# A feed-forward block in split-float32: up projection as Strassen products, down projection as a phase of its own

## The chip, the cores and the metric

The kernel runs on one core of a Trainium2 chip. The metric is the device time of one launch in microseconds (us). The kernel before takes 2258.77 us, the median of two runs (2258.36 and 2259.17).

## The reference

One residual layer over 512 tokens of 2048 channels, in float32: a token mixer with four groups of heads, its output projection and norm, and a feed-forward block. The change lies in the feed-forward and the norm ahead of it:

```python
x = x + rms_norm(y, post_mix_norm[l])
h = rms_norm(x, pre_ffn_norm[l])
y = conv_ffn(h, ffn_up[l], ffn_conv_w[l], ffn_conv_b[l], ffn_down[l])
x = x + rms_norm(y, post_ffn_norm[l])

def conv_ffn(h, up, conv_w, conv_b, down):
    hid = causal_dwconv(h @ up.astype(h.dtype), conv_w, conv_b)      # 3 taps over tokens
    gate, val = jnp.split(hid, 2, axis=-1)                           # 5632 channels each
    return (jax.nn.gelu(gate) * val) @ down.astype(h.dtype)
```

## The kernel before

Every float32 matrix is split into a high and a low part, and a product is three matmuls: high by high, high by low, low by high (`mul3`, L203-207). Weights come in blocks of 128x1024 floats, 512 KB, into one ring of three `raw` buffers (`load`, L160-169, on SP's queue); `split` (L144-158) casts the high part on ACT (`whi`, L155) and subtracts it on DVE (`wlo`, L156), each into four buffers.

The feed-forward has 44 tiles f of 128 gate channels and 44 of value channels. An up tile (`gemm_T`, `up_tile` L894) is 16 row tiles x 3 = 48 matmuls of 128x512 over two raw blocks, each of 8 row tiles of 128 columns, so 512 B in a row. DVE multiplies it by the norm's factor r2 (`fin`, L315), the convolution is one pass on ACT (L330) and two on DVE (L332), then gelu, the product with the gate (L908) and the split of the result into `fh` and `fl`, which stay in SBUF. The first tiles of both kinds go by halves of the tokens (`gemm_half`, L841: matmuls of 128x256), the first halves beside the norm of the last tokens. The norm's residual x1 is transposed on TensorE before r2 is known (L868 to L873); r2 is found meanwhile (`residual_norm`, L879).

The down projection is interleaved: after each group of four f (`up_group`, L901) it multiplies the group before it by ffn_down (`down_cols`, L918), 4 columns of 512 by 4 token tiles, and adds each PSUM bank to a sum in SBUF (L928). `finish` (L947) norms, adds the residual and stores. The order of the instructions on each engine is set by the tile framework's scheduler.

Of the kernel before, what the change touches and what calls it, by code (L numbers as in the profile page):

```python
# [45 lines left out]
# The order in which the mixers' parts are issued: what comes after a part of the DeltaNet fills in  # L46
# where that one waits.
# [9 lines left out]
def trunk(ctx: ExitStack, tc: tile.TileContext, x, xT, cols, rows, gdn_row, sgu_row, w_in, w_ba,  # L57
# [4 lines left out]
    # Slots of one tag are handed out in program order, so work that should run past other work  # L62
    # has tags of its own: G and mm for the DeltaNet, t, acc and fx for what fills in around it.
# [67 lines left out]
    a.activation(out=small([P, 1], "warm"), in_=half[:, 0:1], func=AF.Square)   # its table is loaded early  # L131
# [39 lines left out]
    def load_cols(w, c0):  # L171
        """128 columns, all rows; part (k) -> [P, 128] of hi and lo."""
# [20 lines left out]
    # One buffer of (hi, lo) activations, [channel, token tile, k, token], for h, y and h2 in turn.  # L193
# [9 lines left out]
    def mul3(p, lt, rt, first, last):  # L203
        """p += lt^T rt of (hi, lo) pairs."""
# [18 lines left out]
    def ones_sum(hi, lo, bank):  # L223
        """sums over the partitions of hi + lo, on every partition."""
# [16 lines left out]
    def col_sums(src, bank):  # L241
        """sums over the partitions, tokens on the partitions: [P, token tile]."""
# [19 lines left out]
    # lru_x goes along with the rows of x^T as they come  # L262
# [55 lines left out]
    def tanh_gate(t, zh):  # L318
        """zh holds z/2; gives z * sigmoid(z)."""
# [4 lines left out]
    def conv(dst, src, taps, bias=None):  # L324
        """causal depthwise convolution along the free axis; taps: columns, oldest first."""
# [28 lines left out]
    def softplus(dst, src, shape):  # L354
        """max(x, 0) + log1p(exp(-|x|)), the logarithm as 2 atanh(u / (2 + u))."""
# [112 lines left out]
        # decays  # L468
# [20 lines left out]
        # k k^T and (q k^T)^T  # L489
# [17 lines left out]
        # natural v  # L507
# [6 lines left out]
        # T = (I + M)^-1 by doubling, as its transpose  # L514
# [19 lines left out]
        # the 32nd power as the 16th's twice  # L534
# [10 lines left out]
        # w^T and u  # L545
# [42 lines left out]
    def gdn_norm(h):  # L588
        """x * rsqrt(mean(x^2) + eps) of x = o * rsqrt(P (|q|^2 + eps))"""
# [23 lines left out]
    def norm4(i, tiles):  # L613
        """rms_norm over 4 channel tiles with the i-th group's weight, in place."""
# [221 lines left out]
    # The first two tiles of the feed-forward go by halves of the tokens, the first half before the  # L836
    # last token tile is there.
    def load_up(f):
        return acc("pT"), load_cols(ffn_up, f * P)

    def gemm_half(i, p, wt):  # L841
        ts_ = slice(2 * i, 2 * i + 2)
        for k in range(KD):
            mul3(p[:, i * 2 * P:(i + 1) * 2 * P], wt(k), (act_hi[:, ts_, k, :], act_lo[:, ts_, k, :]),
                 k == 0, k == KD - 1)
# [3 lines left out]
    fetch_x(1)
    for t in range(NTT):  # L850
# [3 lines left out]
        wo_evac(p, t, c, pm)  # L854
        sr = small([P, 1], "sry")
# [5 lines left out]
        if t + 2 < NTT:  # L861
            fetch_x(t + 2)
        if t == NTT - 1:
            first = [gemm_half(0, *load_up(f)) for f in (0, NF)]
        for d in range(DC):
            pt = mm("pt2")
            for j in range(4):
                pe.transpose(pt[:, TS[j]], x1[t][d][:, TS[j]], ident)  # L868
            for j in range(4):
                hh, hl = act_N(4 * d + j, t)  # L870
                sc = col("pre_ffn", 4 * d + j)
                a.activation(out=hh, in_=pt[:, TS[j]], func=AF.Copy, scale=sc)  # L872
                v.scalar_tensor_tensor(out=hl, in0=pt[:, TS[j]], scalar=sc, in1=hh.bitcast(F32),  # L873
                                       op0=ALU.mult, op1=ALU.subtract)
# [1 line left out]
    r2b = new("rb", "r2b")  # L876
    r2 = const.tile([P, NTT], F32, name="r2")

    def residual_norm():  # L879
        for t in range(NTT):  # L880
            for c in range(DC):
                nc.sync.dma_start(out=x1d[TS[t], c * S:(c + 1) * S], in_=x1[t][c])
                junk = waste()
                a.activation(out=junk, in_=x1[t][c], func=AF.Square, accum_out=ss1[:, t, c:c + 1])  # L884
        sr2 = small([P, NTT], "sr2")
        v.tensor_reduce(out=sr2, in_=ss1, axis=mybir.AxisListType.X, op=ALU.add)
        col_rsqrt(r2, sr2, 1.0 / D)
        v.tensor_copy(r2b, to_row(r2, mm))
# [143 lines left out]
```

## Time and profile before

| what | value |
|---|---|
| median of the runs | 2258.77 us |
| span of the profiled execution | 2256.1 us |
| runs' median less the span (launch and end) | 2.7 us |
| TensorE (PE) busy | 2229.6 us, 99% |
| VectorE (DVE), ScalarE (ACT), GpSimd (POOL) busy | 1138.8, 753.2, 104.9 us |
| first matmul of the feed-forward (trace) | 800.72 us |
| last matmul (trace) | 2244.88 us |

All durations of the prediction are from the one profiled execution. In its rows `out<-in` are the program's names; PE is the matmul, PEld the weight load beside it; SPq is SP's DMA queue. Matmuls overlap in the records, so the price of one is read from start to start.

### The profile page before, as it was taken

What the parts mean: (1) busy time and instruction counts of PE and PEld (TensorE: products, weight loads), DVE (VectorE), ACT (ScalarE), POOL (GpSimd) and SP (SyncE); (2) the same over time, 40 slices, a digit from 0 to 9 for tenths busy, and PEclk for the clock granted to TensorE, in tenths of its full rate; (3) what the DMA queues carried; (4) which work ended last, traced back from release to release, by engine and by line L of the source; (5) the groups of instructions that cost most, each with busy time, mean ns of one, the idle gap of its engine ahead of it and who ended that gap; (6) DMA issues with size and microseconds to landing.
All of it is one profiled execution on the core that took longest, in us unless ns stands there. A gap on an engine that the chain in (4) does not pass through costs nothing.

```text
span 2256.1 us, 25143 instructions
## 1 busy us (share of the span) xinstructions
PE 2229.6 (99%) x10260; PEld 1845.3 (82%) x10260; DVE 1138.8 (50%) x1518; ACT 753.2 (33%) x1061; POOL 104.9 (5%) x99
## 2 busy tenths in 40 slices
PE   7999999999999999999999999999999999999998
PEld 6788888888888888888888888888888888888886
DVE  8675453944452474433544445444444444444456
ACT  5464242522332363333223232222323232232323
POOL 6001000100100000000000000000000000000002
PEclk9999999999999999999999999999999999999999
DMA  6222222232243543333333332333333333333352
GB/s 206 72 78 76 66 75 75 78 82 75 84 145 98 168 126 99 94 94 103 90 107 94 96 100 86 106 97 94 103 94 94 98 97 94 103 94 101 96 187 103
DMA packets 308339, 227.13 MB, mean 101 GB/s; under 512 B 8832, under 2 KB 263552, under 8 KB 307712
## 3 DMA queue, kind: packets, MB, share of 16 engines
q1 hardware_dynamic: 303616, 217.15, 33.0%
q10 hardware_dynamic: 4608, 8.39, 1.1%
q8 instruction: 80, 1.31, 0.2%
q14 instruction: 35, 0.29, 0.0%
HBM read 217.12 MB, written 8.39 MB: 100 GB/s over the span
## 4 chain that ended last, share of the span: by engine, by line
issue 63%; PE 31%; ACT 2%; DVE 2%; POOL 1%; DMA 0%; SPq 0%; DVEq 0%; POOLq 0%; ACTq 0%
PE pT L205 5%; PE pT L206 5%; PE pT L207 5%; PE pwo L205 2%; PE pwo L206 2%; PE pwo L207 2%; PE ptt L445 1%; DVE act_lo L280 1%; PE pvs L207 1%; PE pvs L206 1%; PE pvs L205 1%; PE pp L445 1%; PE pss L571 1%; ACT waste L884 0%; DVE wlo L156 0%
## 5 line engine op out<-in xcount | busy, mean ns | idle before, releaser
L205 PE MATMUL pT<-act_hi,whi 128*128 128x512 f32 (+1 forms) x2016 | 781.8, 388 | 1.8 <-ACT act_hi L872 1.8
L206 PE MATMUL pT<-act_lo,whi 128*128 128x512 f32 (+1 forms) x2016 | 781.9, 388 | 0.0
L207 PE MATMUL pT<-act_hi,wlo 128*128 128x512 f32 (+1 forms) x2016 | 780.8, 387 | 0.0
L155 ACT CAST whi<-raw 128x1024 fp32r<-128x1024 f32 x378 | 398.0, 1053 | 1012.3 <-PE pT L206 626.4
L156 DVE TENSOR_TENSOR wlo<-raw,whi 128x1024 fp32r<-128x1024 f32 x378 | 464.5, 1229 | 417.2 <-ACT whi L155 415.7
L205 PEld LDWEIGHTS pT<-act_hi,whi 128*128 128x128 f32 x2016 | 378.5, 188 | 78.9 <-ACT act_hi L872 2.6
L206 PEld LDWEIGHTS pT<-act_lo,whi 128*128 128x128 f32 x2016 | 378.8, 188 | 76.5 <-issue 1.0
L207 PEld LDWEIGHTS pT<-act_hi,wlo 128*128 128x128 f32 x2016 | 378.8, 188 | 76.4 <-issue 1.0
L206 PE MATMUL pd<-wlo,fh 128*128 128x512 f32 x704 | 273.7, 389 | 0.0
L207 PE MATMUL pd<-whi,fl 128*128 128x512 f32 x704 | 273.7, 389 | 0.0
L205 PE MATMUL pd<-whi,fh 128*128 128x512 f32 x704 | 273.5, 389 | 0.0
L315 DVE TENSOR_TENSOR fin<-pT,r2b 128x512 f32<-128x512 f32 x88 | 60.8, 691 | 285.7 <-PE pT L207 285.7
L928 DVE TENSOR_TENSOR facc<-pd,facc 128x512 f32<-128x512 f32 x156 | 107.5, 689 | 132.5 <-PE pd L207 131.8
L206 PEld LDWEIGHTS pd<-wlo,fh 128*128 128x128 f32 x704 | 132.1, 188 | 27.5
L207 PEld LDWEIGHTS pd<-whi,fl 128*128 128x128 f32 x704 | 132.1, 188 | 27.4
L205 PEld LDWEIGHTS pd<-whi,fh 128*128 128x128 f32 x704 | 132.1, 188 | 27.4
L332 DVE SCALAR_TENSOR_TENSOR fcv<-fin,colt,fcv 128x511 f32<-128x511 f32 (+1 forms) x176 | 131.2, 747 | 3.0 <-ACT fcv L330 0.3
L206 PE MATMUL pwo<-wlo,act_hi 128*128 128x512 f32 x224 | 87.1, 389 | 0.0
L207 PE MATMUL pwo<-whi,act_lo 128*128 128x512 f32 x224 | 87.0, 389 | 0.0
L205 PE MATMUL pwo<-whi,act_hi 128*128 128x512 f32 x224 | 86.5, 389 | 0.0
L330 ACT ACTIVATE fcv<-fin,colt 128x512 f32<-128x512 f32 x88 | 71.3, 811 | 1.9 <-DVE fin L315 1.9
L911 ACT CAST fh<-fcv 128x512 fp32r<-128x512 f32 x44 | 27.3, 621 | 122.4 <-DVE fcv L908 122.4
(318 smaller groups left out, 1511.8 us busy)
## 6 DMA issues: line engine op xcount, KB each, us to landing
raw<-in_ffn_up_dram SPq DMA_DIRECT2D x176, 512.0 KB, 4.0
raw<-in_ffn_down_dram SPq DMA_DIRECT2D x88, 512.0 KB, 3.6
raw<-in_w_in_dram SPq DMA_DIRECT2D x86, 512.0 KB, 3.8
raw<-in_w_out_dram SPq DMA_DIRECT2D x32, 512.0 KB, 3.9
xs<-in_xT_dram SPq DMA_DIRECT2D x16, 256.0 KB, 5.3
xr<-in_x_dram ACTq DMA_DIRECT2D x16, 256.0 KB, 5.3
x1d<-yw SPq DMA_DIRECT2D x16, 256.0 KB, 3.6
act_hi<-x1d SPq DMA_DIRECT2D x4, 1024.0 KB, 10.5
```

Of the source, the lines that this page charges most:

```text
L155: a.copy(out=hi, in_=r)
L156: v.tensor_tensor(out=lo, in0=r, in1=hi.bitcast(F32), op=ALU.subtract)
L205: pe.matmul(p, lhsT=lt[0], rhs=rt[0], start=first, stop=False)
L206: pe.matmul(p, lhsT=lt[0], rhs=rt[1], start=False, stop=False)
L207: pe.matmul(p, lhsT=lt[1], rhs=rt[0], start=False, stop=last)
L280: v.scalar_tensor_tensor(out=hl, in0=blk(xs[j]), scalar=col("pre_mix", k), in1=hh.bitcast(F32), op0=ALU.mult, op1=ALU.subtract)
L315: v.tensor_tensor(out=t, in0=p, in1=m, op=ALU.mult)
L330: a.activation(out=dst, in_=src, func=AF.Identity, scale=taps[-1], bias=bias)
L332: v.scalar_tensor_tensor(out=dst[:, j:], in0=src[:, :S - j], scalar=taps[n - 1 - j], in1=dst[:, j:], op0=ALU.mult, op1=ALU.add)
L445: pe.matmul(p[:, TS[t]], lhsT=lhsT[:, TS[t]], rhs=rhs[:, TS[t]], start=True, stop=True)
L911: a.copy(out=ah, in_=vt)
L928: v.tensor_tensor(out=facc[t][c], in0=p, in1=facc[t][c], op=ALU.add)
```

## The change

**Up.** f = 0 to 2 stay plain. From f = 3 on, gate tile f and value tile 44 + f are one product of 2x2 blocks, and Strassen's scheme in its form with 15 additions makes it of 7 block products with 8 row tiles and 256 tokens each: 7 x 8 x 3 = 168 matmuls of 128x256. The four weight blocks are r11 (gate, upper rows), r21 and r22 (value, upper and lower), r12 (gate, lower). Of the four sums of weight blocks, DVE makes s1 = r21 + r22 and s2 = s1 + r11; the other two are made in place by DMAs on GpSimd's queue that read weight rows once more and add them to what stands in the buffer: r21 += gate upper, s2 += gate lower. Each of the 7 blocks is split.

```diff
+    def add_rows(dst, k0, f):
+        nc.gpsimd.dma_start(out=dst.rearrange("p (k n) -> p k n", n=P), accum_op=ALU.add,
+                            in_=ffn_up[k0 * P:(k0 + 8) * P, f * P:(f + 1) * P].rearrange("(k p) n -> p k n", p=P))
+    def up_pair(f):
+        r11, r21, r22, r12 = (load(ffn_up, k0, 8, ff * P, P) for ff, k0 in
+                              ((f, 0), (NF + f, 0), (NF + f, 8), (f, 8)))
+        s1, s2 = B("s1"), B("s2")
+        gs, vs = T("fg"), T("fv")
+        g1, g2, v1, v2 = gs[:, 0:H2], gs[:, H2:], vs[:, 0:H2], vs[:, H2:]
+        add(s1, r21, r22)
+        p1 = product(split(r11), "B11")
+        a.copy(out=v1, in_=p1)
+        add(s2, s1, r11)
+        p5 = product(split(s1), "T1")
+        add_rows(r21, 0, f)
+        p6 = product(split(s2), "T2")
+        add(g2, v1, p6)
+        p2 = product(split(r12), "B21")
+        add(g1, v1, p2)
+        add_rows(s2, 8, f)
+        p7 = product(split(r21), "T3")
+        add(v1, g2, p7)
+        add(v2, v1, p5)
+        add(g2, g2, p5)
+        p4 = product(split(r22), "T4")
+        add(v1, v1, p4)
+        p3 = product(split(s2), "B22")
+        add(g2, g2, p3)
+        gated(f, gs, vs, True)
```

`product` is 8 x `mul3` into a bank of 256 columns, `add` a DVE addition (L984 of the changed kernel), `gated` the convolution, gelu and product, whose result now goes to DRAM (`gd`) by a DMA on GpSimd's queue:

```diff
+        v.tensor_tensor(out=vt, in0=vt, in1=gt, op=ALU.mult)
+        nc.gpsimd.dma_start(out=gd[f * P:(f + 1) * P, :], in_=vt)
+    NPL = 3
...
+    for f in range(NPL, NF):
+        up_pair(f)
```

**Norm.** r2 is found for each token tile and multiplied in before the transposes; `fin` (L315) is gone. The transposed tiles are kept in float32 (`hT`), and DVE and ACT make the sums of activation blocks and their splits from them once, beside f = 1 and 2.

```diff
+        for d in range(DC):
+            a.activation(out=xr[t, d], in_=x1[t][d], func=AF.Copy, scale=r2[:, t:t + 1])
...
-    r2b = new("rb", "r2b")
...
-        s = ev(p, r2b, "fin")
```

**Down.** A phase of its own after all of up: the same 2112 matmuls of 128x512, in two halves of 22 f. The four token tiles of a column hold a PSUM bank each over all 22 f, so an addition in SBUF comes once per bank and not once per group. The first column of each half loads `gd` back and splits it.

```diff
+    for h in range(2):
+        gs = []
+        for c in range(DC):
+            banks = [bank("pd") for _ in range(NTT)]
+            by_k = NH // 2 if h == 0 or c < DC - 1 else 7
+            for i in range(by_k):
+                if c == 0:
+                    gs += [load_g(h * NH + 2 * i + n, 2 * i + n) for n in range(2)]
+                wt = weights(h, i, c)
+                for n in range(2):
+                    k = 2 * i + n
+                    for t in range(NTT):
+                        mul3(banks[t], cut(gs[k], TS[t]), wt[n], k == 0, k == NH - 1)
```

The mixers' buffers are freed before the feed-forward and taken over by a pool of 18 buffers of 1024 floats and 7 of 512; PSUM is regrouped into 8 equal banks. The ring of three `raw` buffers and the four of `whi` and `wlo` stay.

**Order on DVE.** Before, one value tile and one gate tile of the feed-forward, among them 4 splits of weights (`wlo`), in the middle of an up group:

```order
L156 TENSOR_TENSOR wlo_6604<-raw_6601,whi_6603 128x1024
L315 TENSOR_TENSOR fin_6522<-pT_6473,r2b_6212 128x512
L156 TENSOR_TENSOR wlo_6610<-raw_6607,whi_6609 128x1024
L332 SCALAR_TENSOR_TENSOR fcv_6524<-fin_6522,colt_75,fcv_6524 128x511
L332 SCALAR_TENSOR_TENSOR fcv_6524<-fin_6522,colt_75,fcv_6524 128x510
L908 TENSOR_TENSOR fcv_6524<-fcv_6524,fcv_6456 128x512
L912 TENSOR_TENSOR fl_6530<-fcv_6524,fh_6529 128x512
L156 TENSOR_TENSOR wlo_6676<-raw_6673,whi_6675 128x1024
L315 TENSOR_TENSOR fin_6594<-pT_6545,r2b_6212 128x512
L156 TENSOR_TENSOR wlo_6682<-raw_6679,whi_6681 128x1024
L332 SCALAR_TENSOR_TENSOR fcv_6596<-fin_6594,colt_75,fcv_6596 128x511
L332 SCALAR_TENSOR_TENSOR fcv_6596<-fin_6594,colt_75,fcv_6596 128x510
```

After, in the middle of the pairs, from the split of r12 (raw_11637) of one pair to the first sum of the next (s1_11877). raw_11633 is r21, raw_11635 is r22, raw_11631 was r11:

```order
L160 TENSOR_TENSOR wlo_11736<-raw_11637,whi_11735 128x1024
L336 SCALAR_TENSOR_TENSOR fcg_11620<-fg_11403,colt_75,fcg_11620 128x511
L336 SCALAR_TENSOR_TENSOR fcv_11625<-fv_11404,ncv_6206,fcv_11625 128x511
L336 SCALAR_TENSOR_TENSOR fcg_11620<-fg_11403,colt_75,fcg_11620 128x510
L160 TENSOR_TENSOR wlo_11767<-raw_11633,whi_11766 128x1024
L336 SCALAR_TENSOR_TENSOR fcv_11625<-fv_11404,ncv_6206,fcv_11625 128x510
L925 TENSOR_TENSOR fcv_11625<-fcv_11625,fcg_11620 128x512
L160 TENSOR_TENSOR wlo_11799<-raw_11635,whi_11798 128x1024
L984 TENSOR_TENSOR fg_11641<-fv_11642,pT2_11709 128x256
L160 TENSOR_TENSOR wlo_11829<-s2_11640,whi_11828 128x1024
L984 TENSOR_TENSOR fg_11641<-fv_11642,pB21_11739 128x256
L984 TENSOR_TENSOR s1_11877<-raw_11871,raw_11873 128x1024
```

What was a `wlo` every two or three short instructions is now a fixed sequence: three convolution steps stand between the split of r12 and that of r21, which waits for the accumulating DMA too; behind the split of r22 comes the next pair's s1, which reads a buffer that this split frees.

**Order on SP's and GpSimd's queues.** Before, SP's loads of up tiles; GpSimd's instructions from the norm before the feed-forward on (no DMAs):

```order
L166 DMA raw_6539<-in_ffn_up_dram 128x8x128
L166 DMA raw_6601<-in_ffn_up_dram 128x8x128
L166 DMA raw_6607<-in_ffn_up_dram 128x8x128
L166 DMA raw_6673<-in_ffn_up_dram 128x8x128
L166 DMA raw_6679<-in_ffn_up_dram 128x8x128
```

```order
L141 TENSOR_TENSOR ry_5599<-crs_5917,half_82 128x1
L141 TENSOR_TENSOR ry_5599<-crs_6031,half_82 128x1
L141 TENSOR_TENSOR r2_6213<-crs_6360,half_82 128x4
L141 TENSOR_TENSOR rf_15082<-crs_15391,half_82 128x1
L963 TENSOR_TENSOR facc_7398<-facc_7398,act_hi_90 128x512
L963 TENSOR_TENSOR facc_7542<-facc_7542,act_hi_90 128x512
```

After, the four loads of a pair on SP (r11, r21, r22, r12) and two of the next; GpSimd's queue at the same place:

```order
L170 DMA raw_11631<-in_ffn_up_dram 128x8x128
L170 DMA raw_11633<-in_ffn_up_dram 128x8x128
L170 DMA raw_11635<-in_ffn_up_dram 128x8x128
L170 DMA raw_11637<-in_ffn_up_dram 128x8x128
L170 DMA raw_11869<-in_ffn_up_dram 128x8x128
L170 DMA raw_11871<-in_ffn_up_dram 128x8x128
```

```order
L988 DMA raw_11395<-in_ffn_up_dram 128x8x128
L988 DMA s2_11402<-in_ffn_up_dram 128x8x128
L926 DMA gd_6205<-fcv_11387 128x512
L988 DMA raw_11633<-in_ffn_up_dram 128x8x128
L988 DMA s2_11640<-in_ffn_up_dram 128x8x128
L926 DMA gd_6205<-fcv_11625 128x512
L988 DMA raw_11871<-in_ffn_up_dram 128x8x128
L988 DMA s2_11878<-in_ffn_up_dram 128x8x128
```

A pair has four loads for three buffers: r12 takes that of its own r11, the next r11 that of r12, the next r21 and r22 those of r21 and r22. On GpSimd's queue each pair has the accumulate into r21, the one into s2, and the store of the pair's result, where before there was nothing.

## Rows read from the trace of the kernel before

**Rows 1.** The page: busy time by engine, slices of the span, granted clock.
```profile
PE 2229.6 (99%) x10260; PEld 1845.3 (82%) x10260; DVE 1138.8 (50%) x1518; ACT 753.2 (33%) x1061; POOL 104.9 (5%) x99
...
PE   7999999999999999999999999999999999999998
...
PEclk9999999999999999999999999999999999999999
```

**Rows 2.** Window table: span, then PE, PEld, DVE, ACT, POOL busy (count), clock.
```profile
1000.00:1200.00 200.00, 200.00 (x884) 165.59 (x883) 85.50 (x96) 59.52 (x70) 0.00 (x0) 1.00 0.34 98
```

**Rows 3.** Timeline of PE in the first halves: start, duration, instruction.
```profile
805.25 0.28 PE L205 MATMUL pT<-act_hi,whi 128*128 128x256 f32 x1
...
812.81 0.28 PE L205 MATMUL pT<-act_hi,whi 128*128 128x256 f32 x1
```

**Rows 4.** Waits of SP's queue: us in total, times, longest.
```profile
SPq L166 <- DVE wlo L156: 1796.3, 346, 18.0
```

**Rows 5.** Timeline of DVE in the feed-forward.
```profile
1114.65 1.23 DVE L156 TENSOR_TENSOR wlo<-raw,whi 128x1024 fp32r<-128x1024 f32 x1 [0.17 <-ACT whi L155]
1115.79 0.74 DVE L332 SCALAR_TENSOR_TENSOR fcv<-fin,colt,fcv 128x511 f32<-128x511 f32 x1
1116.51 0.69 DVE L928 TENSOR_TENSOR facc<-pd,facc 128x512 f32<-128x512 f32 x1
1117.11 0.74 DVE L332 SCALAR_TENSOR_TENSOR fcv<-fin,colt,fcv 128x510 f32<-128x510 f32 x1
```

**Rows 6.** The page's costliest groups: busy, mean ns of one, idle before.
```profile
L155 ACT CAST whi<-raw 128x1024 fp32r<-128x1024 f32 x378 | 398.0, 1053 | 1012.3 <-PE pT L206 626.4
...
L315 DVE TENSOR_TENSOR fin<-pT,r2b 128x512 f32<-128x512 f32 x88 | 60.8, 691 | 285.7 <-PE pT L207 285.7
...
L330 ACT ACTIVATE fcv<-fin,colt 128x512 f32<-128x512 f32 x88 | 71.3, 811 | 1.9 <-DVE fin L315 1.9
```

**Rows 7.** The page: queues (packets, MB, share); issues (count, KB, us to landing).
```profile
q1 hardware_dynamic: 303616, 217.15, 33.0%
q10 hardware_dynamic: 4608, 8.39, 1.1%
...
raw<-in_ffn_up_dram SPq DMA_DIRECT2D x176, 512.0 KB, 4.0
...
act_hi<-x1d SPq DMA_DIRECT2D x4, 1024.0 KB, 10.5
```

**Rows 8.** Timeline of all engines at one load: cast, subtraction, next issue.
```profile
1025.39 1.05 ACT L155 CAST whi<-raw 128x1024 fp32r<-128x1024 f32 x1 [0.77 <-PE pd L207]
...
1026.47 1.23 DVE L156 TENSOR_TENSOR wlo<-raw,whi 128x1024 fp32r<-128x1024 f32 x1 [7.81 <-ACT whi L155]
...
1027.73 0.37 SPq L166 DMA_DIRECT2D raw<-in_ffn_up_dram  x1
```

**Rows 9.** Timeline of the end: a power, the last matmul, the last store.
```profile
2244.32 0.55 POOL L141 TENSOR_TENSOR rf<-crs,half 128x1 f32<-128x1 f32 x1
...
2244.88 0.39 PE L207 MATMUL pd<-whi,fl 128*128 128x512 f32 x1
...
2252.78 0.33 SPq L967 DMA_DIRECT2D out_dram<-fm  x1
```

**Rows 10.** Timeline of PE from the first half product to the first whole.
```profile
800.72 0.28 PE L205 MATMUL pT<-act_hi,whi 128*128 128x256 f32 x1
...
813.53 1.91 PE L868 MATMUL pt<-ident,yw 128*128 128x128 f32 x16
815.93 0.39 PE L205 MATMUL pT<-act_hi,whi 128*128 128x256 f32 x1 [0.50 <-ACT act_hi L872]
...
830.70 0.39 PE L205 MATMUL pT<-act_hi,whi 128*128 128x512 f32 x1
```

**Rows 11.** The page: weight loads of the up tiles.
```profile
L205 PEld LDWEIGHTS pT<-act_hi,whi 128*128 128x128 f32 x2016 | 378.5, 188 | 78.9 <-ACT act_hi L872 2.6
```

More of the change, by code (lines that the diff above doesn't have):

```diff
@@ L802, in trunk @@
     ssy = const.tile([P, NTT, DC], F32, name="ssy")
+    x1b = [[None] * 2 for _ in range(NTT)]
     x1 = [[None] * DC for _ in range(NTT)]
@@ L819, in trunk, with held_rows @@
             wo_evac(pos[t], t, c, pm)
+    def held_rows(w, k0, c0, held):
+        h = sum((split(r, 1, (lambda n: B(n, F32R)) if held else None) for r in load_raw(w, k0, c0)), [])
+        return lambda i: tuple(side(t, i % 2) for t in h[i // 2])
     c = DC - 1
     pm = row_tile(0, c, "t")
-    spare = ["y"] * NBUF["y"] + ["o"] * NBUF["o"]
-    wts = [load_rows(w_out, order[4 * q], c * S, pick=None if q < 2 else lambda n: new(spare.pop(0), n, F32R))
-           for q in range(4)]
+    wts = [held_rows(w_out, order[4 * q], c * S, q >= 2) for q in range(4)]
     ry = const.tile([P, NTT], F32, name="ry")
+    r2 = const.tile([P, NTT], F32, name="r2")
     ss1 = const.tile([P, NTT, DC], F32, name="ss1")
@@ L843, in gemm_half @@
         for k in range(KD):
[L844 removed]
+            mul3(p[:, i * H2:(i + 1) * H2], wt(k), (act_hi[:, ts_, k, :], act_lo[:, ts_, k, :]),
                  k == 0, k == KD - 1)
         return p, wt
+    hT = [[None] * 2 for _ in range(NTT)]
     fetch_x(0)
[L849 removed]
     for t in range(NTT):
@@ L860, in trunk @@
                                    op0=ALU.mult, op1=ALU.add)
-        if t + 2 < NTT:
-            fetch_x(t + 2)
+            junk = waste()
+            a.activation(out=junk, in_=x1[t][d], func=AF.Square, accum_out=ss1[:, t, d:d + 1])
+            nc.sync.dma_start(out=x1d[TS[t], d * S:(d + 1) * S], in_=x1[t][d])
+        sr2 = small([P, 1], "sr2")
+        v.tensor_reduce(out=sr2, in_=ss1[:, t, :], axis=mybir.AxisListType.X, op=ALU.add)
+        col_rsqrt(r2[:, t:t + 1], sr2, 1.0 / D)
+        for d in range(DC):
+            a.activation(out=xr[t, d], in_=x1[t][d], func=AF.Copy, scale=r2[:, t:t + 1])
         if t == NTT - 1:
-            first = [gemm_half(0, *load_up(f)) for f in (0, NF)]
+            first = [gemm_half(0, acc("pT"), load_cols(ffn_up, f * P)) for f in (0, NF)]
         for d in range(DC):
@@ L877, in trunk @@
[L877 to L888, printed above, removed]
+                pe.transpose(pt[:, TS[j]], xr[t, d][:, TS[j]], ident)
@@ new lines, in trunk @@
+            if d % 2 == 0:
+                hT[t][d // 2] = B("hT")
+            h1 = side(hT[t][d // 2], d % 2)
+            o, _ = _OFF["pre_ffn"]
+            v.tensor_tensor(out=blk(h1), in0=blk(pt), op=ALU.mult,
+                            in1=colt[:, o + 4 * d:o + 4 * d + 4].rearrange("p (k o) -> p k o", o=1)
+                            .broadcast_to([P, 4, P]))
+            hh, hl = (u[:, t, 4 * d:4 * d + 4, :] for u in (act_hi, act_lo))
+            a.copy(out=hh, in_=blk(h1))
+            v.tensor_tensor(out=hl, in0=blk(h1), in1=hh.bitcast(F32), op=ALU.subtract)
@@ new lines, in trunk, with taps, gated @@
+    gd = dr.tile([DFF, S], F32, name="gd")
+    o_cv = _OFF["ffn_conv"][0] + 3 * NF
+    ncv = tp.tile([P, 3 * NF], F32, tag="ncv", name="ncv", bufs=1)
+    v.tensor_scalar_mul(ncv, colt[:, o_cv:o_cv + 3 * NF], -1.0)
+    def taps(f, minus=False):
+        if minus:
+            return [ncv[:, 3 * (f - NF) + i:3 * (f - NF) + i + 1] for i in range(3)]
+        return [col("ffn_conv", 3 * f + i) for i in range(3)]
+    def gated(f, gs, vs, minus):
+        gt = T("fcg")
+        conv(gt, gs, taps(f), bias=col("ffn_cb", f))
+        a.activation(out=gt, in_=gt, func=AF.Gelu_apprx_tanh)
+        vt = T("fcv")
+        conv(vt, vs, taps(NF + f, minus), bias=col("ffn_cb", NF + f))
+        v.tensor_tensor(out=vt, in0=vt, in1=gt, op=ALU.mult)
+        nc.gpsimd.dma_start(out=gd[f * P:(f + 1) * P, :], in_=vt)
@@ L916, in trunk @@
-    facc = [[None] * DC for _ in range(NTT)]
-    def down_cols(parts, c, after=None):
-        wts = [load_rows(ffn_down, gi * FG, c * S) for gi, _ in parts]
-        for t in range(NTT):
-            p = bank4(t)("pd")
-            for i, (_, act) in enumerate(parts):
-                gemm_N(p, lambda k, t: cut(act[k], TS[t]), 0, FG, wts[i], t, i == 0, i == len(parts) - 1)
-            if facc[t][c] is None:
-                facc[t][c] = G("facc")
-                a.copy(out=facc[t][c], in_=p)
-            else:
-                v.tensor_tensor(out=facc[t][c], in0=p, in1=facc[t][c], op=ALU.add)
-            if after is not None:
-                after(t, c)
@@ L932, in trunk @@
-    prev = last = None
-    for gi in range(NG):
-        prev, last = last, (gi, up_group(gi))
-        if prev is not None:
-            for c in range(DC if gi < NG - 1 else DC - 1):
-                down_cols([prev], c)
+    gated(0, first[0][0], first[1][0], False)
+    for j in range(2):
+        b11, b21, b12, b22 = hT[j][0], hT[j][1], hT[j + 2][0], hT[j + 2][1]
+        v.tensor_tensor(out=b22, in0=b22, in1=b12, op=ALU.subtract)
+        v.tensor_tensor(out=b12, in0=b11, in1=b12, op=ALU.subtract)
+        v.scalar_tensor_tensor(out=b11, in0=b11, scalar=-1.0, in1=b22, op0=ALU.mult,
+                               op1=ALU.subtract)
+        v.scalar_tensor_tensor(out=b21, in0=b11, scalar=-1.0, in1=b21, op0=ALU.mult,
+                               op1=ALU.subtract)
@@ new lines, in trunk @@
+    ext = {}
+    for q, t0, i in (("T1", 2, 0), ("T2", 0, 0), ("T3", 2, 1)):
+        ext[q] = [(B("eh", F32R), B("el", F32R)) for _ in range(2)]
+        for j in range(2):
+            for d in range(2):
+                src = side(hT[t0 + j][i], d)
+                eh, el = (side(u, j) for u in ext[q][d])
+                a.copy(out=eh, in_=src)
+                v.tensor_tensor(out=el, in0=src, in1=eh.bitcast(F32), op=ALU.subtract)
+    for f in range(1, NPL):
+        pg, pv = (gemm_T(ffn_up, ff * P) for ff in (f, NF + f))
+        gated(f, pg, pv, False)
@@ new lines, in trunk, with bank, moving @@
+    banks_end.close()
+    ps = ctx.enter_context(tc.tile_pool(name="ps2", bufs=1, space=PSUM, reuse_waits="tile"))
+    def bank(name):
+        return ps.tile([P, S], F32, tag="u", name=name, bufs=8)
+    for j in range(2):
+        src = blk(hT[j][1])
+        eh, el = (u[:, 2 + j, 0:8, :] for u in (act_hi, act_lo))
+        a.copy(out=eh, in_=src)
+        v.tensor_tensor(out=el, in0=src, in1=eh.bitcast(F32), op=ALU.subtract)
+    def moving(q, k):
+        if q in ext:
+            return tuple(u.rearrange("p (j k c) -> p j k c", j=2, k=4)[:, :, k % 4, :] for u in ext[q][k // 4])
+        t0, k0 = {"B11": (0, 0), "B21": (0, 8), "B22": (2, 8), "T4": (2, 0)}[q]
+        return tuple(u[:, t0:t0 + 2, k0 + k, :] for u in (act_hi, act_lo))
@@ new lines, in product, with add @@
+    def product(wt, q):
+        p = bank("p" + q)[:, 0:H2]
+        hi, lo = wt[0]
+        for k in range(8):
+            mul3(p, (hi[:, k * P:(k + 1) * P], lo[:, k * P:(k + 1) * P]), moving(q, k), k == 0, k == 7)
+        return p
+    def add(o, x, y):
+        v.tensor_tensor(out=o, in0=x, in1=y, op=ALU.add)
+    def add_rows(dst, k0, f):
+        nc.gpsimd.dma_start(out=dst.rearrange("p (k n) -> p k n", n=P), accum_op=ALU.add,
+                            in_=ffn_up[k0 * P:(k0 + 8) * P, f * P:(f + 1) * P].rearrange("(k p) n -> p k n", p=P))
@@ new lines, in trunk, with load_g @@
+    for f in range(NPL, NF):
+        up_pair(f)
+    NH = NF // 2
+    GAT = [(0, 0), (0, 1), (1, 0), (1, 1), (0, 2), (0, 3), (1, 2), (1, 3), (2, 2), (2, 3), (3, 2), (3, 3),
+           (2, 0), (2, 1), (3, 0), (3, 1)]
+    def load_g(f, i):
+        gr = T("graw")
+        nc.sync.dma_start(out=gr, in_=gd[f * P:(f + 1) * P, :])
+        if i < 16:
+            t, k = GAT[i]
+            hi, lo = (u[:, t, 4 * k:4 * k + 4, :].rearrange("p k c -> p (k c)") for u in (act_hi, act_lo))
+        else:
+            b = B("gb", F32R)
+            hi, lo = side(b, 0), side(b, 1)
+        a.copy(out=hi, in_=gr)
+        v.tensor_tensor(out=lo, in0=gr, in1=hi.bitcast(F32), op=ALU.subtract)
+        return hi, lo
@@ L940, in trunk, with weights @@
+    fb = [[B("facc") for _ in range(2)] for _ in range(NTT)]
+    facc = [[side(fb[t][c // 2], c % 2) for c in range(DC)] for t in range(NTT)]
+    pf = None
+    def weights(h, i, c):
+        hi, lo = split(load(ffn_down, h * NH + 2 * i, 2, c * S, S))[0]
+        return [(side(hi, n), side(lo, n)) for n in range(2)]
     ssf = const.tile([P, NTT, DC], F32, name="ssf")
     rf = const.tile([P, NTT], F32, name="rf")
-    pf = [row_tile(1, c, "t") for c in range(DC)]
-    x1r = [act_hi[:, t].rearrange("p k c -> p (k c)").bitcast(F32) for t in range(NTT)]
@@ L944, in trunk @@
-    for t in range(NTT):
-        nc.sync.dma_start(out=x1r[t], in_=x1d[TS[t], :])
     def finish(t, c):
@@ L967, in finish @@
             (nc.sync if d % 2 else nc.scalar).dma_start(out=out[TS[t], cs], in_=fd)
-    for c in range(DC - 1):
-        down_cols([last], c, finish)
-    down_cols([prev, last], DC - 1, finish)
+    for h in range(2):
[11 more added lines that the diff above has]
+                        mul3(banks[t], cut(gs[k], TS[t]), wt[n], k == 0, k == NH - 1)
+            if h == 1 and c == DC - 1:
+                x1r = []
+                for t in range(NTT):
+                    x1r.append((act_hi, act_lo)[t % 2][:, t // 2].rearrange("p k c -> p (k c)").bitcast(F32))
+                    nc.sync.dma_start(out=x1r[t], in_=x1d[TS[t], :])
+                wts = [weights(h, i, c) for i in range(by_k, NH // 2)]
+            for t in range(NTT):
+                if h == 1 and c == DC - 1:
+                    for i, wt in enumerate(wts):
+                        for n in range(2):
+                            k = 2 * (by_k + i) + n
+                            mul3(banks[t], cut(gs[k], TS[t]), wt[n], False, k == NH - 1)
+                if h == 0:
+                    a.copy(out=facc[t][c], in_=banks[t])
+                    continue
+                v.tensor_tensor(out=facc[t][c], in0=banks[t], in1=facc[t][c], op=ALU.add)
+                finish(t, c)
+        if h == 0:
+            pf = [row_tile(1, c, "t") for c in range(DC)]
 _ORDER = ["x", "xT", "cols", "rows", "gdn_row", "sgu_row", "w_in", "w_ba", "lru_wa", "lru_wx", "sgu_ws",
```

52 lines of the change are left out of this document (17 added, 35 removed).

## The prediction

> **What bounds the kernel now.** I read the page's busy shares and slices first: the matmul engine is busy 99% of the span, in every slice, at the top level of the granted clock, 2.4 GHz [rows 1]. DVE has half of its time free, ACT two thirds. So a change gains by fewer or shorter matmuls and loses by whatever makes TensorE wait. Next a window table inside the feed-forward, for the price of a matmul: 884 of 128x512 in 200 us, 226.3 ns each [rows 2]. Then the timeline of the one place with 128x256 matmuls: from 805.25 to 812.81 lie 63 of them, 0.120 us each [rows 3]. Half a matmul thus costs 0.53 of a whole one, which eats part of what Strassen saves. Last SP's waits: it waited 1796 us for DVE's `wlo` to free a `raw` buffer [rows 4]. The loads are tied to DVE by a ring of three buffers, which costs nothing today because TensorE has its weights early.
>
> **Matmuls.** Per f, two up tiles are 96 matmuls of 512 columns: 96 x 0.2263 = 21.72 us. A Strassen pair is 7 x 8 x 3 = 168 of 256 columns: 168 x 0.120 = 20.16 us. Over 41 pairs: 41 x 1.56 = **-64.0 us**. The down projection keeps 2112 matmuls of 128x512, and f = 0 to 2 keep theirs: 0.
>
> **DVE and ACT per pair.** From start to next start, DVE takes 1.15 us for a `wlo`, 0.72 for a conv step, 0.60 for a 512-column operation [rows 5]. After the change it has 7 `wlo`, 2 sums of 1024 elements, 4 conv steps, a product and 7 additions of 256 columns: 9 x 1.15 + 4 x 0.72 + 0.60 + 7 x 0.60 at most = 18.0 us, below 20.16. (A 256-column addition is not in these rows; at half price the sum is 15.9.) The two sums that the DMAs make would add 2.3 on DVE and bring it to 20.3, TensorE's own pace. ACT: 7 x 1.05, two of 0.81, and two short ones, about 10.3 us [rows 6]. Neither is a bound as a sum. The multiplication by r2, 88 x 0.69 on DVE [rows 6], goes from under TensorE's cover: 0.
>
> **The new ring of loads.** This is where I expect the loss. The three buffers now serve four loads a pair, in DVE's order. r12 takes r11's buffer, free after s2. Its chain: load 4.0 [rows 7], `whi` 1.05, `wlo` 1.15, three conv steps that stand before the next split on DVE 2.16, `wlo` of r21 1.15, conv step and product 1.32, `wlo` of r22 1.23, which frees the buffer for the next pair's r22: load 4.0, then s1 1.15, `wlo` of r11 1.15, s2 1.23, and r12 may load again. That is 8.0 of loads and 11.6 of DVE and ACT, with 0.2 for hand-overs (0.03 us from ACT to DVE and from DVE to SP in [rows 8]): **19.8 us**, all in series. It is 0.36 below TensorE's 20.16. Queued on SP behind the wait for s2 are all loads of the next pair; on DVE, behind a late `wlo`, the conv, and so the gated tile.
>
> **The accumulating DMAs.** No row shows one, nor any DMA issued by POOL. A 512 KB load takes the 16 engines 33.0% x 2256.1 us x 0.512/217.15 = 1.8 us [rows 7]. An accumulate moves as much and must also read what it adds to: between 1.8 us (a plain load) and 3.6 us (two passes); a gain is excluded, since it is a transfer that is added. It goes out right after s1, 2.4 us before r12's load (the `wlo` of r11 and s2 lie between). At 1.8 its packets are through before r12's come; at 3.6 they are 1.2 us in r12's way, and the ring is 21.0. I take 3.6, because an add without reading its target is impossible and no row gives that second read for less: (21.0 - 20.16) x 41 = **+34.6 us**; both ends, 0 and 34.6, stay in the range.
>
> The Trainium skill, page "DMA: Bandwidth & Descriptors", section "Issuing engines are not separate DMA queues", says that DMAs started by different engines run on the same 16 DMA engines and interleave. The page of this profile shows the SP and ACT queues as shares of the same 16 engines [rows 7], and no run so far shows POOL's; by this rule POOL's queue is no escape for the accumulate, by its opposite the 34.6 us would be nothing.
>
> **Its latency.** The result is wanted by r21's `whi`, which follows, in r12's chain, 9.9 us after s1; the landing rows near it are 4.0 us for the same shape and 10.5 us for 1 MB [rows 7]. Between these ends it just fits. If it lands after A us with A over about 10, the ring runs through it instead: A, `whi`, `wlo`, conv step and product, `wlo` of r22, load, s1 = A + 10.2 us a pair.
>
> **The seams.** The norm's chain ahead of the transposes grows by squares, a sum, a power (0.55 in [rows 9]) and scaled copies, some 3 us, and is covered by 96 half matmuls, 11.5 us. Today this stage, from 800.72 to 830.70, holds 192 x 0.120 = 23.0 us of matmuls and 6.9 us of transposes, sums and waits [rows 10]. The sums and splits of the activations lie beside f = 1 and 2, 43 us of matmuls. In the down phase a weight block with its two g tiles comes every 24 matmuls, 5.4 us, against 4.0 + 1.05 + 1.15 us of latency with three buffers. I take **+5 us**, with -3 (today's waits in the stage gone) and +15 (the 6.9 us twice) as bounds. The gd stores, 0.25 MB a pair, go on POOL's queue behind the accumulates: 0, nobody waits for them until the down phase; if they held the engines as r12's load does, 0.9 us a pair, 37 us. The end, 11.2 us after the last matmul [rows 9], keeps its form: 0.
>
> **Sum.** 2256.1 - 64.0 + 34.6 + 5 = 2231.7 us of span; the median of the runs is 2.7 us above the span: **2234 us**, -1.1%. Its own range is 2215 to 2280 (rings of 20.6 to 22 us, with the seams' bounds).
>
> **Rivals.**
> F, TensorE stays the bound. The accumulate holds the engines under 2.7 us (the 2.4 of lead and the 0.36 of slack), so 20.16 us a pair: 2256.1 - 64.0 + 5 + 2.7 = **2200 us**. For it: a plain load is through in 1.8, the DMA engines are two thirds idle, and TensorE is 99% busy now. Against: a ring with 0.36 us to spare has to keep all its prices.
> S, the accumulate lands late. Place: `whi` of r21, in each of 41 pairs. From A = 12.5 us the pair takes 22.7 and the whole is above 2304; at A = 14 it is 24.2, (24.2 - 20.16) x 41 = 166, and **2366 us**. For it: 1024 short rows of 512 B, each read, added and written, on a queue that the trace has never shown; 1 MB took 10.5 us. Against: a plain load of these rows lands in 4.0, so an accumulate would have to be three times as slow.
> W, half matmuls don't keep 0.120 us, because each loads 128x128 weights first, 188 ns [rows 11]: 168 x 0.188 = 31.6 us a pair, 470 us more, 2670. Against it stand the 63 matmuls at 0.120 [rows 3], each with its load.
>
> The same page of the Trainium skill gives in its section "Anatomy of one DMA — SWDGE (gpsimd) path" a fit for a DMA from that engine; an estimate from it for 512 KB is 3.2 us, by which S would not come. No run so far shows it, and it says nothing of the addition.
>
> **How the numbers follow.** The forecast 0.42, F 0.33, S 0.23, W 0.02. A measurement can tell about 2%, 45 us: faster is below 2213.6, slower above 2303.9. F falls into faster (0.33), the forecast into same (0.42), S and W into slower (0.25). The range leaves out F with seams at their best, below 2194, and the late half of S with W, above 2340.
>
> **What would show it.** Right: in the up stage 168 half matmuls every 21 us, with TensorE at 96% there and its gaps ended by `whi` or `wlo` of r12 or r21; SP's wait at r12 ended by s2, at r22 by the `wlo` of r22; r12's landing later than r11's by about a microsecond. F: no gaps, 20.2 us a pair, the accumulates landing in under 6 us. S: ACT's `whi` of r21 waiting for the accumulate in every pair, and its landing over 12 us. The sum is wrong altogether if the half matmuls start more than 0.125 us apart without a wait, if DVE is above 95% busy in the stage, or if the time is lost in the down phase, where I see no wait.

## The result and the profile after

The changed kernel takes 2316.8 us (median; 2314.9 to 2318.7) against 2258.8: ratio 1.026, 95% interval 1.023 to 1.029. It is slower by 58 us, where 25 us less were forecast. The page of its profiled execution (span 2313.1 us) answers to [rows 1, 7]:

```profile
PE 2211.0 (96%) x13210; PEld 1946.1 (84%) x13210; DVE 1320.3 (57%) x1770; ACT 883.3 (38%) x1203; POOL 260.1 (11%) x228
...
DMA  6222222322242536777777776777777822342224
...
q1 hardware_dynamic: 309952, 228.68, 32.1%
q0 software_dynamic: 88800, 54.53, 16.7%
...
raw<-in_ffn_up_dram SPq DMA_DIRECT2D x176, 512.0 KB, 4.2
...
raw<-in_ffn_up_dram POOLq DMA_DIRECT2D x41, 512.0 KB, 7.5
s<-in_ffn_up_dram POOLq DMA_DIRECT2D x41, 512.0 KB, 6.4
```

TensorE is no longer busy all the time, and over the middle of the span the DMA engines are at seven tenths instead of three. A new queue, q0 (GpSimd's), moves a quarter of what SP's queue (q1) moves, but the times of its packets add up to half as much: its bytes are dear.

The window table over 200 us of pairs (behind the clock stand the DMA engines' share and GB/s), and the waits of SP's queue, answer to [rows 2, 4]:

```profile
1000.00:1200.00 200.00, 185.73 (x1477) 179.44 (x1477) 141.22 (x185) 79.58 (x94) 32.86 (x27) 0.99 0.73 150
```

```profile
SPq L170 <- DVE wlo L160: 1154.8, 267, 18.2
SPq L170 <- DVE s L984: 299.5, 39, 8.9
```

TensorE idles 14 of 200 us at a granted clock of 0.99. The count of matmuls tells the loss better, because their records overlap: 1477 in 200 us, where the unhindered pairs of the first experiment below have 5027 in 600. SP has a wait that was not there before: 39 times for s2, which frees r12's buffer. The chain of waits through one pair shows the whole ring (start, duration, what); its three loads are r22's, r12's and the next r22's:

```profile
1301.27 5.13 DMA raw<-in_ffn_up_dram
...
1307.63 1.22 DVE wlo L160
1308.85 1.15 DVE s L984
...
1310.05 6.29 DMA raw<-in_ffn_up_dram
...
1316.44 1.06 ACT whi L159
...
1318.66 0.74 DVE fcg L336
...
1319.99 0.74 DVE fcg L336
1320.73 1.13 DVE wlo L160
1321.87 0.67 DVE fcv L336
...
1323.24 1.22 DVE wlo L160
...
1324.49 4.41 DMA raw<-in_ffn_up_dram
```

From one r22 load to the next it is 23.2 us here. It is the chain of the prediction, link by link: r22's load, s1, `wlo` of r11, s2, r12's load, `whi`, `wlo`, conv steps, `wlo` of r21 and of r22. Over the chain from 900 to 1720 us, r12's load takes 6.52 us (mean of 33, 6.1 to 7.8) and r22's 4.45 (35). The first and last s1 (867.1 and 1784.3, 40 pairs apart) give 22.93 us a pair. The first of these 40 steps is 28.4 us, while TensorE is busy with the plain tiles until 882.5; the other 39 give 22.79, so 11.8 are left for DVE, ACT and hand-overs. On GpSimd's queue, in the same pair:

```profile
1308.25 1.57 POOL L988 DMA_DIRECT2D raw<-in_ffn_up_dram  x1 [7.23 <-DVE s L984]
1313.96 1.55 POOL L988 DMA_DIRECT2D s<-in_ffn_up_dram  x1 [4.15 <-DVE fg L984]
```

The first accumulate goes out 1.8 us before r12's load and lands 7.7 us after its issue, at 1316.0; r12's lands at 1316.3. Which packets ran when is in the DMA view of three windows, 1308:1310.5, 1310.5:1313 and 1313:1316 (packets; then for each queue packets, MB and share):

```profile
DMA packets 0, 0.00 MB, mean 0 GB/s; under 512 B 0, under 2 KB 0, under 8 KB 0
...
q0 software_dynamic: 727, 0.37, 122.0%
...
q1 hardware_dynamic: 1040, 0.52, 60.3%
q0 software_dynamic: 313, 0.15, 40.6%
```

The accumulate is issued at 1308.25, but none of its packets has started by 1310.5, and r12's load has been issued at 1310.05. Then 727 of the accumulate's 1040 packets run with no packet of r12's among them, and all 1040 of r12's start after 1313. It is the same in the other pairs, by the packet records: the accumulate's first packet starts 2.25 us after its issue (median of 41), 0.5 us after r12's issue, and 79% of its packets start before r12's first one. That one comes 3.15 us after r12's issue, where r11's load needs 1.03. So the accumulate goes mostly ahead of r12's load, and its lead of 1.8 us is spent before it moves anything.

The rest of the loss stands at the two seams, on PE's timeline:

```profile
804.19 0.54 PE L210 MATMUL pT<-act_lo,whi 128*128 128x256 f32 x1 [3.03 <-DVE act_lo L906]
...
822.95 3.67 PE L896 MATMUL pt<-ident,xr 128*128 128x128 f32 x16 [3.99 <-ACT xr L890]
...
838.99 0.40 PE L209 MATMUL pT<-act_hi,whi 128*128 128x512 f32 x1
...
1808.19 0.28 PE L211 MATMUL pB<-act_hi,wlo 128*128 128x256 f32 x1
1815.68 0.80 PE L209 MATMUL pd<-whi,act_hi 128*128 128x512 f32 x1 [7.21 <-ACT act_hi L1035]
...
2300.83 0.40 PE L211 MATMUL pd<-whi,gb 128*128 128x512 f32 x1
```

| stretch of TensorE | before, us | after, us | difference |
|---|---|---|---|
| first half product to first whole tile | 30.0 [rows 10] | 800.7 to 839.0: 38.3 | +8.3 |
| 41 pairs | 41 x 21.72 = 890.5 | 882.5 to 1808.3: 925.8 | +35.3 |
| 2112 matmuls of down | x 0.2263 = 478.0 | 1808.3 to 2301.1: 492.8 | +14.8 |
| last matmul's start to the end | 11.2 [rows 9] | 12.3 | +1.1 |

The pairs begin at 839.0 plus the 43.5 us of f = 1 and 2. The sum, 59.5, is 2.5 above the difference of the spans, because before's 6240 matmuls from the first whole tile on come to 2 us more than 6240 times 0.2263.

### The profile page after: what moved, and what is told of

It is laid out like the page before. It is cut to its first block, busy times and chain, and to the rows that moved or that the text cites. A ratio compares the mean times of both kernels' runs of the same rounds, so it can differ in the third digit from the quotient of the medians.

```text
span 2313.1 us, 32259 instructions
## 1 busy us (share of the span) xinstructions
PE 2211.0 (96%) x13210; PEld 1946.1 (84%) x13210; DVE 1320.3 (57%) x1770; ACT 883.3 (38%) x1203; POOL 260.1 (11%) x228
## 3 DMA queue, kind: packets, MB, share of 16 engines
q0 software_dynamic: 88800, 54.53, 16.7%
## 4 chain that ended last, share of the span: by engine, by line
PE 37%; issue 27%; DMA 18%; DVE 14%; ACT 3%; POOL 1%; SPq 0%; DVEq 0%; ACTq 0%; POOLq 0%
DMA raw<-in_ffn_up_dram 17%; PE pT L210 7%; PE pT L209 7%; PE pT L211 7%; DVE wlo L160 6%; PE pwo L210 2%; PE pwo L211 2%; PE pwo L209 2%; DVE fcg L336 2%; ACT whi L159 2%; DVE s L984 2%; DVE fcv L336 1%; PE ptt L449 1%; PE pvs L211 1%; PE pvs L210 1%
## 5 line engine op out<-in xcount | busy, mean ns | idle before, releaser
L210 PE MATMUL pT<-act_lo,whi 128*128 128x512 f32 (+1 forms) x1032 | 365.0, 354 | 3.2 <-DVE act_lo L906 3.0
L209 PE MATMUL pT<-act_hi,whi 128*128 128x512 f32 (+1 forms) x1032 | 365.2, 354 | 0.0
L211 PE MATMUL pT<-act_hi,wlo 128*128 128x512 f32 (+1 forms) x1032 | 364.1, 353 | 0.0
L211 PE MATMUL pB<-act_hi,wlo 128*128 128x256 f32 x984 | 288.0, 293 | 51.4 <-DVE wlo L160 51.4
L209 PE MATMUL pB<-act_hi,whi 128*128 128x256 f32 x984 | 283.9, 289 | 11.0 <-ACT whi L159 10.7
L211 PE MATMUL pT<-eh,wlo 128*128 128x256 f32 x984 | 280.7, 285 | 0.0
L210 PE MATMUL pB<-act_lo,whi 128*128 128x256 f32 x984 | 279.9, 284 | 0.0
L209 PE MATMUL pT<-eh,whi 128*128 128x256 f32 x984 | 277.1, 282 | 0.0
L210 PE MATMUL pT<-el,whi 128*128 128x256 f32 x984 | 276.9, 281 | 0.0
L209 PE MATMUL pd<-whi,act_hi 128*128 128x512 f32 x512 | 200.6, 392 | 7.2 <-ACT act_hi L1035 7.2
```

Of the source, the lines that this page charges most:

```text
L209: pe.matmul(p, lhsT=lt[0], rhs=rt[0], start=first, stop=False)
L210: pe.matmul(p, lhsT=lt[0], rhs=rt[1], start=False, stop=False)
L211: pe.matmul(p, lhsT=lt[1], rhs=rt[0], start=False, stop=last)
```

## Experiments

**r12 in a buffer of its own.** The pool of s1 and s2 has free buffers; order and the rest stay.

```diff
-        r11, r21, r22, r12 = (load(ffn_up, k0, 8, ff * P, P) for ff, k0 in
-                              ((f, 0), (NF + f, 0), (NF + f, 8), (f, 8)))
+        r11, r21, r22 = (load(ffn_up, k0, 8, ff * P, P) for ff, k0 in ((f, 0), (NF + f, 0), (NF + f, 8)))
+        r12 = B("r12")
+        nc.sync.dma_start(out=r12.rearrange("p (k n) -> p k n", n=P),
...
```

> The ring of three buffers is the theory: r12's load (6.5 us) and the next r22's (4.4 us) stand in series with 12.0 us of DVE and ACT, 22.95 us a pair. With r12 in a buffer of its own it no longer waits for s2, nor the next r11 for it, and TensorE is the bound again at 20.2 us a pair: 41 x 2.75 = 113 us less than the changed kernel, about 2204 us (2198 to 2215). Rival, the accumulate's own landing (7 us after its issue, ahead of r21's split) sets the pair: then nothing changes, 2310 to 2320.

Measured: 2210.2 us, ratio to before 0.979 (0.977 to 0.980). The window table:

```profile
1000.00:1600.00 600.00, 600.00 (x5027) 600.00 (x5026) 490.19 (x631) 288.98 (x331) 110.85 (x90) 1.00 0.85 172
```

No wait is left in the pairs, and r12's load still takes 6.2 us: with nobody waiting for it, that costs nothing. The pairs lie from 882.9 to 1705.4, 20.06 us each. So the series of waits is the loss, and the accumulate's landing is not. The 6 us beyond the centre of the expectation are its own arithmetic: 22.95 was read from s1 to s1, but TensorE, which starts the first pair 15 us behind its s1, takes 925.8 / 41 = 22.58 a pair and had lost only 22.58 - 20.06, 103 us in all.

**An eighth of each accumulate.**

```diff
-        nc.gpsimd.dma_start(out=dst.rearrange("p (k n) -> p k n", n=P), accum_op=ALU.add,
-                            in_=ffn_up[k0 * P:(k0 + 8) * P, f * P:(f + 1) * P].rearrange("(k p) n -> p k n", p=P))
+        nc.gpsimd.dma_start(out=dst[:, 0:P], accum_op=ALU.add, in_=ffn_up[k0 * P:(k0 + 1) * P, f * P:(f + 1) * P])
```

> Each accumulating DMA adds only one of its eight row tiles, 64 KB instead of 512; order and waits stay (the sums are incomplete). If the accumulate's packets are what stretches r12's load from about 4 to 6.5 us, that load falls to 4.0 to 4.2 and the pair to 12.0 + 4.2 + 4.2 = 20.4 us: about 2212 us (2200 to 2225). Rival, r12's load is slow for another reason (its buffer, the queue on SP): it keeps 6.5 us and the time stays above 2300.

Measured: 2212.9 us, 0.980 (0.979 to 0.982). From the page and the window table:

```profile
q0 software_dynamic: 15328, 16.92, 3.6%
...
raw<-in_ffn_up_dram SPq DMA_DIRECT2D x176, 512.0 KB, 4.0
```

```profile
1000.00:1600.00 600.00, 599.61 (x5020) 599.27 (x5019) 479.70 (x627) 280.58 (x330) 68.27 (x90) 1.00 0.46 124
```

The ring of three alone costs almost nothing: 0.4 of 600 us. It is the accumulate's size, its packets in r12's way, that pushes the ring past TensorE.

**The same DMAs without the addition.**

```diff
-        nc.gpsimd.dma_start(out=dst.rearrange("p (k n) -> p k n", n=P), accum_op=ALU.add,
+        nc.gpsimd.dma_start(out=dst.rearrange("p (k n) -> p k n", n=P),
```

> The same two DMAs on GpSimd's queue without the addition: they overwrite the buffer, same bytes, order and waits. If reading the target and adding is what makes an accumulate hold the DMA engines for about 4.2 us instead of a load's 1.8, r12's load falls to between 4.2 and 5.2 us, the pair to 20.6 to 21.6 us, and the time to 2215 to 2262 us. Rival, it is the second transfer as such, from GpSimd's queue, whatever it does: r12 keeps 6 us or more and the time stays above 2295.

Measured: 2257.1 us, 0.9997 (0.9985 to 1.0008), between the two others and inside the first range. From its page:

```profile
q0 software_dynamic: 15328, 54.53, 7.9%
...
raw<-in_ffn_up_dram POOLq DMA_DIRECT2D x41, 512.0 KB, 4.7
```

Same bytes on q0, less than half of the packets' time. In the chain r12's load takes 5.09 us (mean of 35) and r22's 4.49, and first and last s1 are 861.6 us apart, 21.54 a pair; without the first step, again 28.4, it is 21.37, and 11.8 are left for the rest, as above. Of the 2.5 us by which r12's load is above 4.0, 1.1 come with a second transfer as such and 1.4 with the addition. The edit changes more than the arithmetic, though: q0 has 15328 packets instead of 88800, 128 of 4 KB for each plain transfer where an accumulate has 1024 of 512 B, and the first packet starts 1.6 us after the issue instead of 2.25. Size alone is not the price: the packets of SP's loads are of 512 B too and take 28 ns each, the accumulate's 67.

**No pairs at all.**

```diff
-    NPL = 3
+    NPL = NF
```

> No Strassen pair: all 44 f plain, two tiles of 48 matmuls of 512 columns, the rest of the change (norm ahead of the transposes, gd through DRAM, down as a phase of its own) kept. The theory puts 113 us of the result into the pairs' waits, -64 into their matmuls and only some 8 us into the seams: 2258.8 + 8 = about 2267 us (2258 to 2275). Rival, the down phase or the seams hold a large part of the loss: above 2290.

Measured: 2280.2 us, 1.010 (1.008 to 1.011): a miss. On q0 only the 44 stores of g are left:

```profile
q0 software_dynamic: 3520, 11.54, 1.3%
```

The new norm and the separate down phase cost 22 us, not 8. With that, Strassen's own worth can be read: 2280.2 less 2210.2 is 70 us, 1.7 a pair, a little over the forecast 64 (the half matmul is 0.1193 us, 5027 in 600).

**All four sums on DVE, the ring of three kept.** The weight rows that the DMAs read once more stand in r11 and r12 anyway.

```diff
-        add_rows(r21, 0, f)
+        add(r21, r21, r11)
...
-        add_rows(s2, 8, f)
+        add(s2, s2, r12)
```

> The ring of three buffers stays as in the changed kernel, but DVE makes all four sums: r21 += r11 and s2 += r12 from the buffers that are there anyway. No accumulating DMA is left. DVE then has 16.3 + 2 x 1.15 = 18.6 us a pair. The chain from r12's load to r22's load and back: two loads of about 4.1, and by this kernel's order on DVE 11.4 us of sums, splits and convolution steps: 19.7 us, just under TensorE's 20.04. If the accumulates were the whole of the loss, the time is that of the kernel with r12 in a buffer of its own: 2210 us (2205 to 2235). Rival, the sums were put on DMAs because DVE can't carry them beside the ring: 21.5 us a pair or more, above 2270.

Measured: 2210.5 us, 0.979 (0.978 to 0.980).

```profile
1000.00:1600.00 600.00, 600.00 (x5027) 600.00 (x5027) 551.95 (x691) 284.79 (x330) 16.20 (x30) 1.00 0.40 119
```

DVE is at 92% and TensorE never waits. The rival, that DVE can't carry the sums, is out, and the DMA engines are at 0.40 where they were at 0.73.

**Both together.** The edits of the first and the fifth experiment.

> All four sums on DVE, and r12 in a buffer of its own, so that the ring has a few microseconds to spare. TensorE is the bound at 20.04 us a pair; the accumulating DMAs were worth nothing if this is 2210 us, as with them (2205 to 2216). Rival, DVE at 18.6 of 20.04 us can't keep up with the order of the splits and TensorE waits: 2225 or more.

Measured: 2211.7 us, 0.980 (0.978 to 0.981). Once TensorE is the bound, neither a fourth buffer nor the place of the sums adds anything.

**The start of the down phase.** On top of r12's own buffer:

```diff
         up_pair(f)
+        if f == NF - 2:
+            for i in range(2):
+                e = B("ge")
+                for n in range(2):
+                    nc.sync.dma_start(out=side(e, n), in_=gd[(2 * i + n) * P:(2 * i + n + 1) * P, :])
+                    early.append(side(e, n))
...
```

> r12 in a buffer of its own, and the first four g tiles of the down phase are loaded from DRAM into two free buffers ahead of the last pair's loads, so that TensorE need not wait at the start of the down phase (5.1 us there, and about 4 us more at half the granted clock right after it). Theory: 2210 less 5 to 9, 2201 to 2206. Rival, the down weights are what is late there and the wait stays: 2209 to 2212.

Measured: 2202.6 us, 0.976 (0.974 to 0.977). No wait between the last pair and the down phase is left; the g tiles were late, queued on SP behind weights that waited for the ring.

**One more small buffer at the norm.** On top of that:

```diff
-    NBUF = {"t": 7}
+    NBUF = {"t": 8}
```

> As the kernel before this one (r12 in a buffer of its own, first g tiles early), with 8 instead of 7 buffers of 512 floats, so that one more tile of x is loaded ahead of the last token tile's norm. Theory: the first wait at the norm (3.5 us in that kernel, ended by a subtraction that DVE does behind a wait for a tile of x) comes from the missing buffer and goes or shrinks: 2198 to 2201 us. Rival, the wait is set by the load's own time or by the order around it and stays: 2202 to 2204.

Measured: 2194.6 us, 0.972 (0.971 to 0.974), the best of all, 2.8% below the kernel before, and below the expected 2198 to 2201. PE's waits in the norm stage are now

```profile
816.41 2.50 PE L896 MATMUL pt<-ident,xr 128*128 128x128 f32 x16 [1.73 <-ACT xr L890]
820.78 0.39 PE L210 MATMUL pT<-act_lo,whi 128*128 128x256 f32 x1 [1.52 <-DVE act_lo L906]
...
832.21 0.40 PE L209 MATMUL pT<-act_hi,whi 128*128 128x512 f32 x1
```

The first wait, for a tile of x, is gone as expected, but the gain, 8 us, is more than that wait's 3.5. The scheduler also put the transposes of the third token tile earlier, and the clock did not fall (last section). How much each of these gave was not taken apart.

## Why the prediction was wrong

- Matmuls, -64.0: right. 168 of 0.1193 us, 20.06 us a pair in the first experiment, against 20.16.
- DVE, at most 18.0 a pair: right as a bound, and unnecessarily wide. A 256-column addition takes 0.33 us from start to start (1311.37, 1311.70, 1312.03 in the changed kernel), so the sum is 16.1; and "the two sums that the DMAs make ... bring it to 20.3, TensorE's own pace" came out at 18.4 (the fifth experiment's 92% of 20.04). That was the argument for the accumulates, and it doesn't hold.
- The ring, "19.8 us, all in series": right in every link but its two loads. DVE, ACT and hand-overs are 11.8, as forecast; the wait at r12 is ended by s2, TensorE's gaps by `whi` or `wlo`.
- **The step that failed** is what the accumulate puts in r12's way: "It goes out right after s1, 2.4 us before r12's load [...] At 1.8 its packets are through before r12's come; at 3.6 they are 1.2 us in r12's way, and the ring is 21.0". Measured it is 2.5 us: r12's load is 6.52 and not 5.2. The lead is the term that is shown wrong. The accumulate is issued 1.8 us before r12's load, not 2.4, and its packets start about 0.5 us after that load's issue, so hardly anything of it is through by then. The third experiment bears this out: its plain transfer, at the 1.8 us at which nothing should have been in r12's way, still costs 1.1 us there.
- The size, 3.6 with two passes as the upper bound, is left open. q0 took 16.7% of 2313.1 us for 82 accumulates and the 44 stores of g; the stores alone take 1.3% of 2279.0 in the kernel without pairs. That makes 4.35 us of packet time on 16 engines for one accumulate, and by the same reckoning 1.82 for a plain transfer in the third experiment. But the packets overlap in the records (122% of 16 engines above), so 4.35 is not a time for which the engines are held; the middle four fifths of an accumulate's packets start within 2.5 us. How the 1.3 us beyond the forecast 1.2 divide between lead and size was not taken apart.
- r22's load, forecast 4.0, is 4.45: in the pair shown it is issued 0.9 us behind the pair's gd store and 2.6 us behind r21's load, and both land after that. The stores stood at 0 in the prediction; no run leaves them out. 11.8 + 6.5 + 4.45 is the measured 22.8, and TensorE's pairs, forecast 29.4 us faster, are 35.3 slower: 65 us.
- **The seams**, +5 with +15 as the outer bound: +24 (8.3, 14.8 and 1.1), confirmed by the 22 us of the kernel without pairs. "I see no wait" in the down phase was wrong: its g tiles stand in SP's queue behind down weights that wait for `raw` buffers, 7.2 us, with matmuls at half the granted clock behind (0.50 from 1816 to 1820 us). These 19 us and the 65 make up the miss of 83, to 1 us.
- F: its condition, engines held under 2.7 us, counts on the same lead of 2.4 and was not enough: the plain transfers of the third experiment are at 1.8, and the pair still takes 21.4 us and the whole 2257. In the first, second, fifth and sixth experiment, where nothing stands in r12's way or nobody waits for it, the time is within 13 us of its 2200.
- S: its side and its time (above 2304) came true by luck, the mechanism did not. The accumulate lands in 7.5 us, not 12, and r21's split isn't what waits: its `whi` starts at 1318.8 in the pair shown, 2.8 us after the landing.
- W: out, by the same 0.1193 us.
- The sum adds up to 2234, but the prediction's own range does not follow from its terms: a ring of 20.6 with -3 gives 2210 and one of 22 with +15 gives 2285, not 2215 and 2280, and the end of 0 for the accumulates, said to stay in, gives 2200. The measured time is outside either way.
- The Trainium skill, "DMA: Bandwidth & Descriptors", section "Issuing engines are not separate DMA queues", says the engines are shared and the transfers interleave. Here the trace agrees on the sharing: r12's load takes 6.5 us beside a full accumulate, 5.1 beside a plain transfer. Of interleaving it shows little: 79% of the accumulate's packets start before r12's first. The estimate of 3.2 us from the same page's fit is not borne out for these transfers: 4.7 us plain, 7.5 with the addition.

## What to carry to other kernels

A ring of few buffers turns loads into links of a series: add up load, cast, subtraction and whatever the engine does in between, and if the sum comes near the bound engine's pace, a microsecond more on a load is paid in every round, as here. An operation moved from a half-idle engine to a DMA is not free when the next load shares the DMA engines with it. Count its lead from its first packet and not from its issue, and set the rest of its packets against the slack of the loads beside it. A buffer taken from a pool that has one spare was worth more (107 us) here than Strassen itself (70).

## What was not expected of the hardware

The packets of an accumulating DMA of 512 KB in rows of 512 B took 4.35 us of 16 engines, 2.4 times the 1.82 of a plain transfer of the same rows from the same queue (which has fewer and larger packets); it landed in 7.5 us instead of 4.7. Its first packet started 2.25 us after its issue, against 1.6 for the plain one and 1.0 for r11's load on SP's queue.

A short wait of TensorE costs more than its length. The window table of the changed kernel around the waits of 3.0 and 4.0 us at the norm (the third number from the end of a row is the granted clock):

```profile
800.00:804.00 4.00, 1.16 (x6) 0.62 (x4) 1.45 (x3) 2.53 (x5) 0.00 (x0) 1.00 1.01 340
804.00:808.00 4.00, 3.81 (x19) 3.81 (x20) 3.59 (x10) 1.76 (x6) 0.03 (x1) 0.57 0.80 258
808.00:812.00 4.00, 4.00 (x35) 4.00 (x35) 2.09 (x4) 3.42 (x7) 1.03 (x2) 1.00 0.53 191
...
824.00:828.00 4.00, 3.87 (x19) 3.58 (x18) 3.90 (x6) 3.77 (x8) 0.00 (x0) 0.50 0.02 4
```

After the wait the clock stood at 1.2 GHz, half of its upper level, for about 4 us: 19 matmuls instead of 35 in a window. In the last experiment, with waits of 1.7 and 1.5 us in the same stage, the granted clock stayed at 1.00:

```profile
812.00:820.00 8.00, 5.54 (x41) 4.45 (x39) 7.31 (x13) 5.91 (x12) 1.53 (x1) 1.00 0.01 2
820.00:828.00 8.00, 7.22 (x59) 7.21 (x60) 8.00 (x13) 6.23 (x10) 0.00 (x0) 1.00 0.00 0
```
